# Second output projection of a two-layer encoder: where the normalisation's factors and offsets are loaded, and where the last row block's transposes stand

## The chip, the cores and the metric

One core of a Trainium2 chip. TensorE (PE) multiplies matrices and transposes blocks, VectorE (DVE), ScalarE (ACT) and GpSimd (POOL) do the element work, SyncE (SP) issues transfers. The metric is the device time of one execution in microseconds (us); the time of a kernel is the median over its runs.

## The reference

A trunk of two layers over 1024 frames with 1024 features, all in float32. Layer 0 mixes tokens by latent attention, layer 1 by differential attention; each mixer is followed by a normalised residual, then a SwiGLU feed-forward part (hidden size 2816) with another.

```python
def _swiglu(x, w_gu, w_down):
    gate, up = jnp.split(x @ w_gu, 2, axis=-1)
    return (jax.nn.silu(gate) * up) @ w_down

for i in range(DEPTH):              # DEPTH = 2
    mix = ...                       # i = 0: latent attention; i = 1: differential attention,
                                    # 8 heads, o normalised per head, then o @ w_o
    h = _layernorm(ALPHA * h + mix, ln_mix_g[i], ln_mix_b[i])
    h = _layernorm(ALPHA * h + _swiglu(h, ffn_w_gu[i], ffn_w_down[i]), ln_ffn_g[i], ln_ffn_b[i])
```

The change lies at the end of layer 1's mixer: the product `o @ w_o`, the first normalisation with `ln_mix_g[1]` and `ln_mix_b[1]`, and the start of layer 1's feed-forward part.

## The kernel before

The 1024 frames are eight row blocks of 128. float32 products are made of rounded halves: an operand is split into a high and a low part (`op_unit`: a cast on ScalarE, L517, then a difference on VectorE or POOL, L518), and TensorE makes three products, high by high, high by low and low by high.

**Attention's last head and the output projection.** Attention goes head by head. Within a head and row block there are scores `s_b` (L220) for two softmax maps; `l_b` holds the logits, exponentials (L228, ScalarE) and, after the reciprocal `rb` (L1442), the scaling on POOL (L1443) and the difference of the two maps (L1444, VectorE), the attention weights. These are transposed by TensorE into `pt_b` (L148), split into `pth_b` and `ptl_b` (L251, L252), and multiplied with the values into `o_b` (L263). The last head takes the row blocks in the order `LAST_ORDER = (6, 7, 4, 5, 2, 3, 0, 1)`.

`OutProj` makes `o @ w_o` for these blocks. Its constructor loads the split weights of the eight heads: `who`/`wlo` for heads 0 and 1 (L376), and one tile `wo_2` to `wo_7` of 1 MB each for the others (L370), all from SP. `of` loads the transposed `o` of six heads for a block (L388), `load_z` the residual `z_a` (L412). For blocks 6 and 7 the product `zp_a` (L431) with heads 0 to 5 runs early, between the last head's rows; the rest runs when that head is done. `rest` normalises each block with `gb`, a tile that holds factors and offsets broadcast to all 128 partitions (0.5 MB each; L176 multiplies by the factors, L184 adds the offsets), and then `raw_x` transposes the block into the feed-forward part's operand (`xTp_a`, eight 128x128 transposes per block in two tiles). The last block's `raw_x` is returned by `rest` as a function, and is called by the feed-forward part.

**The start of the feed-forward part.** Its first products are the gate columns: `load` fetches gate operands `gp_n` from SP (L577) and combined ones `gr_n` (L571), `prepare` and `op_unit` make operands of them, and `consume` multiplies: product "1" then "2" of column group n into the accumulator `ga_n` (L561). After "1" ScalarE copies the accumulator (L628), after "2" it applies SiLU (L630), and the accumulator's bank is free for another group; ga_2 takes that of ga_0.

**What sets the order.** The program is written in dependency order, and a scheduler that works with planned durations of instructions and transfers sets the order on every engine; each engine then executes its list in order. `behind(i, j)` adds a bare order: instruction i is planned behind j. A queue on SP executes its issues in order; each transfer has a semaphore out of a ring of eight, so an issue can wait for the transfer eight issues back.

Of the kernel before, what the change touches and what calls it, by code (L numbers as in the profile page):

```python
# [16 lines left out]
P = 128  # L17
# [21 lines left out]
LAST_ORDER = (6, 7, 4, 5, 2, 3, 0, 1)  # L39
# [3 lines left out]
def trunk(  # L43
# [32 lines left out]
    nc = tc.nc  # L76
    V, A, G, T = nc.vector, nc.scalar, nc.gpsimd, nc.tensor
# [4 lines left out]
    ident = cp.tile([P, P], F32, tag="ident", name="ident")  # L82
# [24 lines left out]
    def f32(t):  # L107
        return t.bitcast(F32)

    def big_tile(name, dt=F32R):  # L110
        return big.tile([P, 2, 1024], dt, tag="big", name=name)

    def ps_s(name):
        return ps.tile([P, 512], F32, tag="s", bufs=ps_bufs[0], name=name)

    def ps_m(name):
        return ps.tile([P, 512], F32, tag="m", bufs=ps_bufs[1], name=name)
# [27 lines left out]
            T.matmul(ps_out, ll, rh, start=False, stop=(i == n - 1))  # L145

    def tr(ps_out, in_):
        T.transpose(ps_out, in_, ident)  # L148

    def bcast_row(pool, src, n, name, tag):  # L150
        t = pool.tile([P, n], F32, tag=tag, name=name, bufs=1)
# [3 lines left out]
    def behind(i, j):  # L155

        tc.add_manual_dep(
            i, j.name,
            mybir.DependencyInfo(mybir.DependencyClass.NoSync, mybir.DependencyReason.DATA),
            reason="kept in program order",  # L160
        )
# [46 lines left out]
    ends = {}  # L208
# [140 lines left out]
    class OutProj:  # L349
# [5 lines left out]
        def __init__(self, side, w_dr, o_dram, o_here, x_src, x_dst, scale):  # L355
            self.st = ExitStack()
            self.pool = self.st.enter_context(tc.tile_pool(name="op1", bufs=2, side=side, reuse_waits="tile"))
            self.o_dram, self.o_here, self.x_src, self.x_dst, self.scale = o_dram, o_here, x_src, x_dst, scale
            self.oh, self.z, self.sums, self.m, self.loaded = {}, {}, {}, {}, {}
            self.of(LAST_ORDER[0])  # L360
            self.wo = []
            for h in range(H):
                if h == 6:
                    self.load_z(LAST_ORDER[0])
                if h == self.HEADS:
                    self.of(LAST_ORDER[1])
                    self.load_z(LAST_ORDER[1])
                if h > 1:
                    t = self.pool.tile([P, 2, D], F32, tag=f"wo{h}", name=f"wo1_{h}", bufs=1)
                    nc.sync.dma_start(t, w_dr[h])  # L370
                    t = t.bitcast(F32R)
                    self.wo.append((t[:, 0], t[:, 1]))
                else:
                    t = [wp.tile([P, D], F32, tag=f"w{p}", name=f"w{p}o1_{h}") for p in "hl"]
                    for p in range(2):
                        nc.sync.dma_start(t[p], w_dr[h][:, p])  # L376
                    self.wo.append([x.bitcast(F32R) for x in t])
# [80 lines left out]
        def rest(self, lng, lnb, xo):  # L458
            gb = big_tile("gb1", F32)
            for i, src in enumerate((lng, lnb)):  # L460
                nc.gpsimd.dma_start(gb[:, i], src.partition_broadcast(P))
            prev = None
            for tb in LAST_ORDER:
                if tb not in LAST_ORDER[:2]:
                    self.of(tb)
                if tb != LAST_ORDER[0]:
                    self.late(tb)
                z = self.z[tb]
                layer_norm(z, self.sums[tb], [self.m[tb, nh] for nh in range(2)], z, gb[:, 0], gb[:, 1],
                           f"a1_{tb}", self.x_dst[tb * P:(tb + 1) * P, :])  # L470
                if prev is not None:
                    raw_x(self.z[prev], xo, prev, f"a1_{prev}")
                prev = tb
            self.st.close()
            return lambda: raw_x(self.z[prev], xo, prev, f"a1_{prev}")

    def raw_x(y, xo, tb, name):

        c = slice((tb % 4) * P, (tb % 4) * P + P)
        pvs = []
        for kh in range(2):
            pt = ps_s(f"xTp_{name}_{kh}")
            for k in range(4):
                tr(pt[:, k * P:(k + 1) * P], y[:, (4 * kh + k) * P:(4 * kh + k + 1) * P])
            pv = pt.rearrange("p (k t) -> p k t", k=4)
            pvs.append(pv)
            if tb >= 4:
                hi, lo = (t[:, :, c] for t in xo[kh, 0])  # L490
                A.copy(hi, pv)
                V.tensor_tensor(lo, pv, f32(hi), ALU.subtract)
                A.copy(xo["r", kh, 0][:, :, c], pv)
        if tb < 4:
            b11, b12, b21, b22 = (xo["r", k, t][:, :, c] for k in range(2) for t in range(2))
            V.tensor_tensor(b12, pvs[0], b11, ALU.subtract)
            A.copy(b22, pvs[1])
            V.tensor_tensor(b11, b22, pvs[0], ALU.subtract)
            V.tensor_tensor(b21, b21, pvs[1], ALU.subtract)
            ends["x"] = V.tensor_tensor(b21, b21, b12, ALU.add).ins  # L500
# [33 lines left out]
    def ffn(side, xo, xst, pending, layer, x_src, x_dst, lng, lnb, next_x, spare=()):  # L534
# [15 lines left out]
        r, tmp, ops, acc, hp, pg, early_cast = {}, {}, {}, {}, {}, {}, {}  # L550
        pg_dr = dr.tile([npre // 2, P, 4, 512], F32, name=f"pg_dr{layer}")

        def p1g0(n):


            t, i = (tmp[n], 2) if n in tmp and n > 1 else (pg[n // 2], 2 * (n % 2))
            return t[:, i], t[:, i + 1]

        def product(o, w, x, first):
            return [  # L560
                T.matmul(  # L561
                    o, w[:, a, k * P:(k + 1) * P], x[b][:, k, :], start=(first and k == 0 and (a, b) == (0, 0)),
                    stop=(k == 3 and a == 1), skip_group_check=True,
                ).ins for k in range(4) for a, b in ((0, 0), (0, 1), (1, 0))
            ]
# [50 lines left out]
        def consume(n, pr):  # L616


            w, nm_ = ops.pop((n, pr)), f"{layer}_{n}"
            if pr in "12":  # L620
                if pr == "1":
                    acc[n, "a"] = ps_s(f"ga{nm_}")
                    if n >= npre:
                        new_tmp(n)
                product(acc[n, "a"], w, xo["12".index(pr), 0], pr == "1")
                p1, g0 = p1g0(n)
                if pr == "1":
                    ends["p1"] = A.copy(p1, acc[n, "a"]).ins  # L628
                else:
                    A.activation(g0, acc[n, "a"], AF.Silu)  # L630
                return
            if pr in "53":
                if pr == "5" or n < 2:
                    acc[n, "c"] = c = (ps_s if n == 1 else ps_t)(f"gc{nm_}{pr}")
                    acc.setdefault((n, "cs"), []).append(c)
                i = product(acc[n, "c"], w, xs["t1" if pr == "5" else "b22"], pr == "5" or n < 2)
                if n == NFF - 1 and pr == "5":
                    behind(i[0], ends["7"])
                if n < 2:
                    return  # L640
            else:
                if pr == "6":
                    acc[n, "b"] = ps_m(f"gb{nm_}")
                    if n < npre:
                        new_tmp(n)
                ends[pr] = product(acc[n, "b"], w, xs[{"6": "t2", "7": "t3", "4": "t4"}[pr]], pr == "6")[-1]
            u2, u3 = tmp[n][:, 0], tmp[n][:, 1]
            p1, g0 = p1g0(n)
            if pr == "6":
                V.tensor_tensor(u2, p1, acc[n, "b"], ALU.add)  # L650
                for c in acc[n, "cs"] if n < 2 else ():
                    V.tensor_tensor(u2, u2, c, ALU.add)
            elif pr == "7":
                V.tensor_tensor(u3, p1, acc[n, "b"], ALU.add)
                if n < 2:
                    V.tensor_tensor(u3, u3, acc[n, "cs"][0], ALU.add)
            elif pr == "5":
                V.tensor_tensor(u3, u3, acc[n, "c"], ALU.add)
            elif pr == "4":
                V.tensor_tensor(p1, p1, acc[n, "b"], ALU.add)  # L660
            else:
                V.tensor_tensor(u2, u2, acc[n, "c"], ALU.add)
            if n == NFF - 1 and pr == "3":
                held.append((n, u2, u3, p1, g0))
            elif pr == ("4" if n < 2 else "3"):
                activations(n, u2, u3, p1, g0)
# [360 lines left out]
        else:  # L1027
            gb = big_tile(f"gb_{nm}", F32)
# [11 lines left out]
            for t in range(4):  # L1040
                y = yb[t // 2][:, t % 2]
# [4 lines left out]
            for t in range(4):  # L1046
                y = yb[t // 2][:, t % 2]
# [297 lines left out]
    xo, stacks = x_pools("m0", "right")  # L1345
# [16 lines left out]
    with ExitStack() as st:  # L1362
# [11 lines left out]
        for ql in q_lo:  # L1374
            for mp in range(2):
                b = slice(64 - mp * 64, 128 - mp * 64)
                z = bb[b, :512]
                i = G.tensor_tensor(ql[b, mp * 512:mp * 512 + 512], z, z, ALU.subtract).ins
# [169 lines left out]
    xo, stacks = x_pools("m1", "left")  # L1548
# [92 lines left out]
```

## Time and profile before

| | us |
|---|---|
| median of 3 runs (2258.09 to 2258.78) | 2258.73 |
| the profiled execution's own time | 2259.4 |
| its span in the profile | 2257.6 |
| TensorE busy | 2236.1 |
| VectorE, ScalarE, POOL busy | 1543.2, 1013.5, 773.6 |
| mean granted TensorE clock, share of full | 0.999 |

The profile's rows carry engine, line, operation and tile, written out<-in; numbers that tell apart the tiles of one name are left out (`wo` is wo_2 to wo_7). "Idle before, <-releaser" is the time for which an engine waited ahead of an instruction, and what ended it. PEld is TensorE's loading of weights, which overlaps its products. q1 is the queue of transfers that SP issues, q0 that of POOL's.

### The profile page before, as it was taken

How to read it: one execution, taken by the hardware profiler on the slowest of the kernel's cores; microseconds unless marked ns; L12 is line 12 of the kernel's file. 1: busy time of each engine (PE TensorE's matmuls, PEld its weight loads, DVE VectorE, ACT ScalarE, POOL GpSimd, SP SyncE). 2: the span in 40 equal slices, each digit the busy share in tenths (PEclk: the TensorE clock that was granted, in tenths of full speed). 3: DMA queues.
4: the chain of work that ended last, by engine and by line, in shares of the span. 5: the costliest groups of instructions: out<-in, count | busy, mean ns of one | idle time of the engine just before them, and what ended most of it. 6: DMA issues, size and time to landing. Idle time of an engine off the chain costs nothing.

```text
span 2257.6 us, 31061 instructions
## 1 busy us (share of the span) xinstructions
PE 2236.1 (99%) x11410; PEld 1912.8 (85%) x11410; DVE 1543.2 (68%) x2894; ACT 1013.5 (45%) x2097; POOL 773.6 (34%) x626
## 2 busy tenths in 40 slices
PE   8999999999999999999999999999999999999998
PEld 8999998888888888888889898988888888888886
DVE  5676765696666657767576666577787666658778
ACT  4455664352333334445465656455532333334444
POOL 2232341114434440456432424222014444430561
PEclk9999999999999999999999999999999999999999
DMA  5010125434435338454311212063344232238443
GB/s 204 14 35 32 42 71 187 142 129 148 178 126 204 118 131 326 177 200 150 103 44 33 64 34 68 24 224 131 121 150 163 80 113 98 103 114 324 164 182 149
DMA packets 105545, 287.76 MB, mean 127 GB/s; under 512 B 7968, under 2 KB 30112, under 8 KB 94896
## 3 DMA queue, kind: packets, MB, share of 16 engines
q1 hardware_dynamic: 101552, 277.44, 34.5%
q0 software_dynamic: 3840, 8.33, 1.4%
q8 instruction: 90, 1.47, 0.3%
q14 instruction: 63, 0.52, 0.1%
HBM read 204.47 MB, written 77.07 MB: 125 GB/s over the span
## 4 chain that ended last, share of the span: by engine, by line
PE 96%; DVE 1%; ACT 1%; DMA 1%; issue 0%; POOL 0%; SPq 0%; DVEq 0%; POOLq 0%
PE gb L561 16%; PE gc L561 10%; PE ga L561 10%; PE dw L885 8%; PE dx L885 5%; PE zp_a L431 4%; PE s_a L220 4%; PE s_b L220 3%; PE dv L885 3%; PE dy L885 3%; PE bp L145 3%; PE bp L143 3%; PE bp L144 3%; PE o_a L263 2%; PE o_b L263 2%; PE hq L1136 2%
## 5 line engine op out<-in xcount | busy, mean ns | idle before, releaser
L517 ACT CAST op_g<-gr 128x512 fp32r<-128x512 f32 x240 | 146.7, 621 | 378.3 <-PE gb L561 190.0
L518 POOL TENSOR_TENSOR op_g<-gr,op_g 128x512 fp32r<-128x512 f32 x104 | 145.9, 1408 | 254.5 <-ACT op_g L517 142.1
L518 DVE TENSOR_TENSOR op_h<-rh,op_h 128x512 fp32r<-128x512 f32 x152 | 140.6, 951 | 51.5 <-ACT op_h L517 51.5
L561 PE MATMUL ga<-xh_m,op_g 128*128 128x512 f32 x512 | 168.3, 389 | 0.0
L885 PE MATMUL dw<-op_w_t,op_h 128*128 128x512 f32 x660 | 151.1, 390 | 0.0
L517 ACT CAST op_h<-rh 128x512 fp32r<-128x512 f32 x152 | 91.9, 619 | 127.6 <-PE dx L885 35.3
L885 PEld LDWEIGHTS dw<-op_w_t,op_h 128*128 128x128 f32 x660 | 123.7, 188 | 25.6
L228 ACT ACTIVATE l_b<-l_b,mx_b 128x256 f32<-128x256 f32 (+7 forms) x128 | 99.4, 777 | 74.8 <-DVE mx_b L223 73.0
L518 POOL TENSOR_TENSOR op_w_b<-rw_b,op_w_b 128x512 fp32r<-128x512 f32 x44 | 64.4, 1486 | 172.6 <-ACT op_w_b L517 172.6
L518 DVE TENSOR_TENSOR op_g<-gr,op_g 128x512 fp32r<-128x512 f32 x136 | 111.7, 824 | 17.3 <-ACT op_g L517 17.0
L885 PE MATMUL dx<-op_w_b,op_h 128*128 128x512 f32 x528 | 121.5, 390 | 1.0 <-DVE op_w_b L518 1.0
L1443 POOL TENSOR_SCALAR l_b<-l_b,rb,cst 128x128 f32<-128x128 f32 (+3 forms) x64 | 52.5, 821 | 200.6 <-DVE rb L1442 189.2
L885 PEld LDWEIGHTS dx<-op_w_b,op_h 128*128 128x128 f32 x528 | 98.8, 188 | 23.0 <-DVE op_w_b L518 2.6
L561 PE MATMUL gb<-t2h_f,op_g 128*128 128x512 f32 x352 | 115.5, 390 | 0.4 <-DVE op_g L518 0.4
L561 PE MATMUL gc<-t1h_f,op_g 128*128 128x512 f32 x352 | 115.7, 390 | 0.0
L561 PE MATMUL gb<-t4h_f,op_g 128*128 128x512 f32 x352 | 115.6, 389 | 0.0
L561 PE MATMUL gc<-b22h_f,op_g 128*128 128x512 f32 x352 | 115.4, 389 | 0.0
L561 PE MATMUL gb<-t3h_f,op_g 128*128 128x512 f32 x352 | 115.2, 389 | 0.0
L561 PEld LDWEIGHTS ga<-xh_m,op_g 128*128 128x128 f32 x512 | 96.1, 188 | 20.0
L518 POOL TENSOR_TENSOR op_g<-s,op_g 128x512 fp32r<-128x512 f32 x40 | 55.0, 1375 | 166.3 <-ACT op_g L517 158.3
L143 PE MATMUL bp<-xT_f,h_wb 128*128 128x512 f32 x256 | 101.9, 398 | 0.0
L144 PE MATMUL bp<-xT_f,h_wb 128*128 128x512 f32 x256 | 101.6, 397 | 0.0
(388 smaller groups left out, 6690.7 us busy)
## 6 DMA issues: line engine op xcount, KB each, us to landing
gr<-in_w_gu SPq DMA_DIRECT2D x44, 1024.0 KB, 6.8
rh<-h_dr SPq DMA_DIRECT2D x28, 1024.0 KB, 5.0
h_dr<-sh SPq DMA_DIRECT2D x22, 1024.0 KB, 5.0
h_dr<-hp SPq DMA_DIRECT2D x22, 768.0 KB, 4.1
tt<-in_w_dn SPq DMA_DIRECT2D x22, 512.0 KB, 7.4
rh<-h_dr SPq DMA_DIRECT2D x12, 768.0 KB, 4.3
wo_dr<-op_pwo SPq DMA_DIRECT2D x16, 512.0 KB, 3.4
z<-xs_dr SPq DMA_DIRECT2D x16, 512.0 KB, 10.4
```

Of the source, the lines that this page charges most:

```text
L143: T.matmul(ps_out, lh, rh, start=(i == 0), stop=False)
L144: T.matmul(ps_out, lh, rl, start=False, stop=False)
L145: T.matmul(ps_out, ll, rh, start=False, stop=(i == n - 1))
L220: T.matmul(s[:, :w], lh, rh[:, ks], start=(j == 0), stop=(j == len(q_pass) - 1))
L228: ends["exp"] = A.activation(l[:, :n], l[:, :n], AF.Exp, bias=mx, scale=-1.0, accum_out=sm).ins
L263: T.matmul(po[:, c], a, b[:, j % 2, c], start=st, stop=sp_, skip_group_check=True)
L431: T.matmul(m, a[:, h, :], self.wo[h][w][:, c], start=(start and h == heads[0] and a is oh and w == 0), stop=(stop and h == heads[-1] and a ...
L517: turns["cast"] = A.copy(hi, src).ins
L518: return eng.tensor_tensor(lo, src, f32(hi), ALU.subtract).ins
L561: T.matmul(o, w[:, a, k * P:(k + 1) * P], x[b][:, k, :], start=(first and k == 0 and (a, b) == (0, 0)), stop=(k == 3 and a == 1), skip_gro ...
L885: T.matmul(o, h[:, a, c], w[:, b_], start=(first and (a, b_) == (0, 0)), stop=(last and a == 1), skip_group_check=True,).ins for a, b_ in ...
L1443: G.tensor_scalar(l1[:, :n], l1[:, :n], r[:, 1:2], nlam, ALU.mult, ALU.mult)
```

## The change

Two things. The two loads of `gb` are issued by SP instead of POOL, planned behind the load of the last weight, which the constructor keeps in `last_w`. And the transposes of the last block in `LAST_ORDER` (block 1) are planned behind the last product of gate group 0, product "2", which `consume` keeps in `ends["gate"]`.

```diff
     def tr(ps_out, in_):
-        T.transpose(ps_out, in_, ident)
+        return T.transpose(ps_out, in_, ident).ins
...
-                    nc.sync.dma_start(t, w_dr[h])
+                    self.last_w = nc.sync.dma_start(t, w_dr[h]).ins
...
         def rest(self, lng, lnb, xo):
             gb = big_tile("gb1", F32)
             for i, src in enumerate((lng, lnb)):
-                nc.gpsimd.dma_start(gb[:, i], src.partition_broadcast(P))
+                behind(nc.sync.dma_start(gb[:, i], src.partition_broadcast(P)).ins, self.last_w)
...
             for k in range(4):
-                tr(pt[:, k * P:(k + 1) * P], y[:, (4 * kh + k) * P:(4 * kh + k + 1) * P])
+                i = tr(pt[:, k * P:(k + 1) * P], y[:, (4 * kh + k) * P:(4 * kh + k + 1) * P])
+                if tb == LAST_ORDER[-1]:
+                    behind(i, ends["gate"])
...
-                product(acc[n, "a"], w, xo["12".index(pr), 0], pr == "1")
+                i = product(acc[n, "a"], w, xo["12".index(pr), 0], pr == "1")[-1]
+                if (n, pr) == (0, "2"):
+                    ends["gate"] = i
```

`raw_x` and `consume` serve both layers. The order of layer 0 and of all up to layer 1's last head is the same before and after; the scheduler makes another order of that head's end and of the start of the second feed-forward part. The last block's transposes stand in both orders between ga_0's product "2" and ga_1's.

On SP, at the output weights (the first number after a name is that of the head or row block). Before:

```order
L412 DMA z_a_7_14972<-xs_dr_98 128x1024
L370 DMA wo_6_14975<-wo_dr_95 128x2048
L370 DMA wo_7_14977<-wo_dr_96 128x2048
L388 DMA of_a_4_15581<-o_dr_2_87 128x6x128
L388 DMA of_a_5_15672<-o_dr_2_87 128x6x128
L412 DMA z_a_4_15584<-xs_dr_98 128x1024 x2
```

After; the two loads of `gb` stand between the last weight and the first load of `o`:

```order
L412 DMA z_a_7_14972<-xs_dr_98 128x1024
L370 DMA wo_6_14975<-wo_dr_95 128x2048
L370 DMA wo_7_14977<-wo_dr_96 128x2048
L461 DMA gb_15518<-in_ln_mix_g 128x1024
L461 DMA gb_15518<-in_ln_mix_b 128x1024
L388 DMA of_a_4_15581<-o_dr_2_87 128x6x128
L388 DMA of_a_5_15672<-o_dr_2_87 128x6x128
```

Both wait for semaphores of transfers only, those of wo_2 and wo_3; the two `of` loads behind them now wait for those of wo_4 and wo_5.

On TensorE, at the end of the last head, where block 3's attention weights are transposed. Before:

```order
L220 MATMUL s_b_1_1_0_15377<-bk_10192,bq_10189 128x256
L220 MATMUL s_b_1_1_0_15377<-bk_10192,bq_10190 128x256
L148 MATMUL pt_b_3_0_15386<-ident,l_b_3_0_15262 128x128 x4
L431 MATMUL zp_a_6_0_6_15467<-wo_6_14975,oh_a_6_14948 128x512 x2
L431 MATMUL zp_a_6_1_6_15475<-wo_6_14975,oh_a_6_14948 128x512 x2
L1474 MATMUL ms_2_0_15395<-sq_2_15363,ones 128x256
```

After; the transposes of block 3 are now followed by two short instructions, and the output products come behind those:

```order
L220 MATMUL s_b_1_1_0_15377<-bk_10192,bq_10189 128x256
L220 MATMUL s_b_1_1_0_15377<-bk_10192,bq_10190 128x256
L148 MATMUL pt_b_3_0_15386<-ident,l_b_3_0_15262 128x128 x4
L1478 MATMUL ms_2_0_15395<-sq_2_15363,ones 128x256
L148 MATMUL pt_b_0_0_15414<-ident,l_b_0_0_15334 128x128
L431 MATMUL zp_a_6_0_6_15467<-wo_6_14975,oh_a_6_14948 128x512 x2
```

Further up, the 18 products of `zp_a` for block 7's first half now stand ahead of that block's transposes `pt_b_7_0`; before, behind them.

On ScalarE at the same place, the exponentials of block 3 and the cast of block 2's transposes. Before:

```order
L228 ACTIVATE l_b_3_0_15262,smb_3_15260<-l_b_3_0_15262,mx_b_3_0_0_15266 128x512
L1477 ACTIVATE sq_3_15258<-ms_3_0_15293,cst 128x256
L251 CAST pth_b_4_1_15238<-pt_b_5_0_15279 128x2x128
L228 ACTIVATE l_b_3_1_15269,smb_3_15260<-l_b_3_1_15269,mx_b_3_1_0_15273 128x512
L1479 ACTIVATE sq_3_15258<-sq_3_15258 128x256
L251 CAST pth_b_2_0_15355<-pt_b_2_0_15351 128x2x128
```

After; the cast of `pt_b_2_0` comes ahead of the second exponential of block 3:

```order
L228 ACTIVATE l_b_3_0_15262,smb_3_15260<-l_b_3_0_15262,mx_b_3_0_0_15266 128x512
L1483 ACTIVATE sq_0_15169<-sq_0_15169 128x512
L1481 ACTIVATE sq_3_15258<-ms_3_0_15293,cst 128x256
L251 CAST pth_b_2_0_15355<-pt_b_2_0_15351 128x2x128
L228 ACTIVATE l_b_3_1_15269,smb_3_15260<-l_b_3_1_15269,mx_b_3_1_0_15273 128x512
L1483 ACTIVATE sq_3_15258<-sq_3_15258 128x256
```

On ScalarE at the start of the second feed-forward part. Before:

```order
L628 COPY pg_0_16137<-ga_0_16163 128x512
L628 COPY pg_0_16137<-ga_1_16177 128x512
L517 CAST op_gp_3_1_16219<-gp_3_16217 128x512
L630 ACT_TABLE_LOAD
L630 ACTIVATE pg_0_16137<-ga_0_16163 128x512
L517 CAST op_gp_3_2_16222<-gp_3_16217 128x512
L497 COPY xr_m_15515<-xTp_a_1_1_16234 128x4x128
L517 CAST t1h_f_16303<-xr_m_15517 128x512 x4
L517 CAST op_gp_4_1_16320<-gp_4_16318 128x512
```

After; the first cast of gp_4 stands ahead of the table load and ga_0's SiLU, where it stood behind the four casts of t1h:

```order
L632 COPY pg_0_16137<-ga_0_16163 128x512
L632 COPY pg_0_16137<-ga_1_16177 128x512
L519 CAST op_gp_3_1_16219<-gp_3_16217 128x512
L519 CAST op_gp_4_1_16320<-gp_4_16318 128x512
L634 ACT_TABLE_LOAD
L634 ACTIVATE pg_0_16137<-ga_0_16163 128x512
L519 CAST op_gp_3_2_16222<-gp_3_16217 128x512
L499 COPY xr_m_15515<-xTp_a_1_1_16234 128x4x128
```

On SP there, the load of gp_4 now stands ahead of those of gr_0 and gr_1, and behind them before.

## The prediction

> **What bounds the kernel now.** I read the page first, for which engine sets the end; then TensorE's waits around the change; then the stretches, the queues and the single rows there. The page, with columns of busy us, share of the span and instructions, and below it the chain that ended last:
>
> ```profile
> span 2257.6 us, 31061 instructions
> PE 2236.1 (99%) x11410; PEld 1912.8 (85%) x11410; DVE 1543.2 (68%) x2894; ACT 1013.5 (45%) x2097; POOL 773.6 (34%) x626
> PE 96%; DVE 1%; ACT 1%; DMA 1%; issue 0%; POOL 0%; SPq 0%; DVEq 0%; POOLq 0%
> ```
>
> TensorE is idle for 2257.6 − 2236.1 = 21.5 us of the whole program, so no change that leaves its instructions alone can win more. Next, its waits from 1480 to 1700 us, the second output projection and the start of the second feed-forward part, where the change acts (us in total, times, longest):
>
> ```profile
> PE zp_a L431 <- DMA wo<-wo_dr: 1.2, 1, 1.2
> PE pt_b L148 <- DVE l_b L1444: 1.2, 2, 0.9
> PE zp_a L431 <- DVE ol_a L420: 0.4, 1, 0.4
> ```
>
> Four stalls of 2.8 us together: that is the most that can be gained here. One, 1.2 us, is a wait for an output weight. The stretches round it (us, then busy us of PE, PEld, DVE, ACT, POOL, then clock, DMA share, GB/s):
>
> ```profile
> 1490.00:1496.00 6.00, 6.00 (x38) 5.24 (x36) 5.75 (x16) 4.17 (x10) 2.32 (x3) 1.00 0.94 349
> 1496.00:1500.00 4.00, 2.82 (x13) 2.03 (x12) 1.84 (x5) 1.00 (x2) 0.00 (x0) 1.00 1.02 427
> 1500.00:1510.00 10.00, 10.00 (x66) 8.89 (x65) 7.40 (x22) 5.68 (x13) 2.11 (x2) 1.00 1.02 424
> ```
>
> The transfer engines are full from 1490 on, and where TensorE stalls, VectorE and ScalarE starve too (1.84 and 1.00 of 4 us). So a stall removed here moves the whole tail of the attention forward.
>
> **The change part by part: the factors and offsets.** The issues on SP and POOL (start, duration, queue, line), the transfers' packets between 1490.0 and 1497.8, the times to landing of `gb` and of the first wide weight (wo_2, issued 1488.49), and the stall:
>
> ```profile
> 1488.49 2.01 SPq L370 DMA_DIRECT2D wo<-wo_dr  x4
> 1497.83 9.05 SPq L388 DMA_DIRECT2D of_a<-o_dr  x2
> 1490.59 0.59 POOL L461 DMA_DIRECT2D gb<-in_ln_mix_g  x1 [5.78 <-PE bv L145]
> 1491.18 0.54 POOL L461 DMA_DIRECT2D gb<-in_ln_mix_b  x1
> ...
> q1 hardware_dynamic: 430, 2.40, 81.6%
> q0 software_dynamic: 116, 0.48, 14.8%
> gb<-in_ln_mix_g POOLq DMA_DIRECT2D x1, 512.0 KB, 9.1
> gb<-in_ln_mix_b POOLq DMA_DIRECT2D x1, 512.0 KB, 12.2
> ...
> wo<-wo_dr SPq DMA_DIRECT2D x1, 1024.0 KB, 9.3
> ...
> 1497.81 0.74 PE L431 MATMUL zp_a<-wo,oh_a 128*128 128x512 f32 x2 [1.18 <-DMA wo<-wo_dr]
> ```
>
> wo_2 lands at 1488.5 + 9.3 = 1497.8, just when TensorE starts again. In the 7.8 us before, `gb` took 0.48 MB, or 14.8% of 7.8 us = 1.15 us of all 16 engines. Behind the last weight it takes none of that, so wo_2 lands 1.15 us sooner and the stall of 1.18 us all but goes: −1.15 us. Ends: 0 if wo_2 doesn't land sooner, −1.2 if the stall goes altogether. The later weights gain more (all of `gb`, 1.05 MB at 424 GB/s, is 2.5 us), so the next one isn't what is late then.
>
> [...]
>
> What the two issues pass: POOL loses 1.13 us of issuing, in an idle stretch (5.78 us idle before it): nothing. On SP they come behind wo_7 and, as each reuses the semaphore of the transfer eight issues back, wait for wo_2 and wo_3 to land; behind them stand the two `of` loads, issued from 1497.83 before, now some 6 us later. The landing time of the first `of` load, and the first uses of `of` and of `gb`:
>
> ```profile
> of_a<-o_dr SPq DMA_DIRECT2D x1, 384.0 KB, 17.9
> ...
> 1534.31 0.94 ACT L419 ACTIVATE oh_a<-of_a,cst 128x768 fp32r<-128x768 f32 x1
> ...
> 1543.99 1.28 DVE L176 SCALAR_TENSOR_TENSOR z_a<-z_a,nmu_a,gb 128x1024 f32<-128x1024 f32 x1
> ```
>
> The engines are full and the bytes the same, so the last of them lands when it did before, at about 1497.8 + 17.9 = 1515.7; some 18 us are left for `of`, 28 us for `gb`. Nothing on the path. If that cover were gone, each us of lateness would be a us of VectorE, then of TensorE.
>
> **The order of the attention's tail.** The schedule is made anew: the last head's rows stand otherwise. First a row of such products for their pace (2.89 us for 12), then the stalls that are there, and the chain that feeds the largest (l_b_3: exponential, reciprocal, POOL's scaling, VectorE's difference):
>
> ```profile
> 1613.80 2.89 PE L431 MATMUL zp_a<-wo,oh_a 128*128 128x512 f32 x12
> ...
> 1512.29 0.63 PE L148 MATMUL pt_b<-ident,l_b 128*128 128x128 f32 x4 [0.30 <-DVE l_b L1444]
> 1531.70 0.52 PE L148 MATMUL pt_b<-ident,l_b 128*128 128x128 f32 x3
> 1535.12 0.66 PE L148 MATMUL pt_b<-ident,l_b 128*128 128x128 f32 x4 [0.85 <-DVE l_b L1444]
> 1537.99 0.50 PE L431 MATMUL zp_a<-wo,ol_a 128*128 128x512 f32 x1 [0.41 <-DVE ol_a L420]
> ...
> 1531.85 0.74 ACT L228 ACTIVATE l_b<-l_b,mx_b 128x512 f32<-128x512 f32 x1
> 1533.05 0.77 POOL L1443 TENSOR_SCALAR l_b<-l_b,rb,cst 128x512 f32<-128x512 f32 x1 [1.52 <-DVE rb L1442]
> 1533.86 1.21 DVE L1444 SCALAR_TENSOR_TENSOR l_b<-l_b,rb,l_b 128x512 f32<-128x512 f32 x1 [0.15 <-POOL l_b L1443]
> ```
>
> At pt_b_7_0 (1512.29) the 18 products of zp_a_7_0 now stand ahead of it, 18 × 0.24 = 4.3 us: the stall of 0.30 goes. At pt_b_3_0 ScalarE now takes the cast of pt_b_2_0 ahead of l_b_3's second exponential; so that exponential starts some 0.75 us behind pt_b_2_0's start (0.5 for its transposes, 0.25 for the cast), and pt_b_3_0 follows 1535.12 − 1531.85 = 3.27 us behind the exponential: 4.0 us. TensorE had 1535.12 − 0.85 − 1531.70 = 2.57 us of work between the two, and has two more score products now, 2.8 us. Stall 1.2 us; up to 2.1 if other work in ScalarE's queue delays the exponential further. pt_b_2_0 itself has less ahead of it: 0 to 0.5 us. The 0.41 stays. Net −0.30 − 0.85 + (1.2 to 2.1) + (0 to 0.5): I take +0.5, near the middle; the ends are −1.15, if both old stalls go and none comes, and +1.45.
>
> **The start of the feed-forward part.** The hold on block 1's transposes sets them behind ga_0's second product, where they stood. Their input is ready at 1623.95 and they start at 1625.58 with no idle time: 0. But around them ScalarE's cast of gp_4 moves from behind the block's casts to ahead of its table load and ga_0's SiLU. Row by row: the block's normalisation and transposes, SP's issue of gp_4, ScalarE, VectorE's first use of a gr load, TensorE where ga_1 ends and ga_2 begins, and the landing times of all six gp (min, median, max), then that of gp_3:
>
> ```profile
> 1622.67 1.28 DVE L184 SCALAR_TENSOR_TENSOR z_a<-z_a,rs_a,gb 128x1024 f32<-128x1024 f32 x1
> 1625.58 1.03 PE L148 MATMUL xTp_a<-ident,z_a 128*128 128x128 f32 x8
> 1622.82 0.33 SPq L577 DMA_DIRECT2D gp<-in_w_gu  x1
> 1624.18 1.28 ACT L630 ACT_TABLE_LOAD   x1
> 1625.78 0.60 ACT L630 ACTIVATE pg<-ga 128x512 f32<-128x512 f32 x1 [0.32 <-PE ga L561]
> 1629.35 0.62 ACT L517 CAST op_gp<-gp 128x512 fp32r<-128x512 f32 x1
> 1630.53 0.69 DVE L598 TENSOR_TENSOR gr<-gr 128x512 f32<-128x512 f32 x1
> 1628.96 0.61 PE L561 MATMUL ga<-xh_m,op_gp 128*128 128x512 f32 x2
> ...
> DMA to landing us min/median/max: 3.7/4.9/6.7
> ...
> gp<-in_w_gu SPq DMA_DIRECT2D x1, 512.0 KB, 4.4
> ```
>
> gp_4 can't be issued before 1622.82 (SP waits there for VectorE to free its buffer). If it lands at L, the cast, the table load and the SiLU end at L + 0.05 + 0.62 + 1.28 + 0.60 + 0.05 = L + 2.6. ga_2 takes ga_0's accumulator, which that SiLU frees, and TensorE wants it with the second product of the row at 1628.96, at 1629.2. gp_3 had a wide gr load right behind it, as gp_4 has now, so I take its 4.4 us: L = 1627.2, ga_2 at 1629.8, stall 0.6 us. Ends: 3.7 gives none, 6.7 gives 2.9. The two gr loads, once ahead of gp_4, now go behind it, from about 1623.2; VectorE takes the first at 1630.53, 7.3 us on, and what it does ahead of that waits for gp_4's cast by then, so a late gr costs VectorE a little and TensorE nothing yet.
>
> [...]
>
> **Sum.** −1.15 + 0.5 + 0.6 = −0.05 us. The profiled execution took 2259.4 us for its span of 2257.6, 0.67 over the median of 2258.73; taken from the median, 2258.7 us. The ends add up to −1.2 − 1.15 + 0 = −2.35 and 0 + 1.45 + 2.9 = +4.35, that is 2256.4 to 2263.1.
>
> **The rivals.**
> - The weight's wait goes and nothing takes its place: gp_4 lands within 3.8 us, and the tail costs nothing or gains. −1.15, to −2.35 with the old stalls gone: 2256.4 to 2257.6. For it: a landing of 3.7. Against: five of six gp landings are longer.
> - The move does nothing, because wo_2 lands no sooner: +0.5 + 0.6, 2259.8. Against it: the DMA share of 0.94 to 1.02.
> - Slower: ScalarE stands at gp_4's cast, and ga_2 with it. It decides from L = 1626.6, a landing of 3.8 us. With the slowest, 6.7: −1.15 + 0.5 + 2.9 = +2.25, 2261.0. To be slower by over 0.2%, which is 4.5 us and about what a measurement of this kernel tells from no change, it takes a landing of 8.9 us. Only if gp_4's share goes to the gr load behind it is that possible.
>
> **How the numbers follow.** The forecast, two small stalls for one: 0.52. Nothing in its place: 0.22. No effect on wo_2: 0.12. The cast's stall at over 2 us: 0.12, of which 0.05 beyond 0.2%. Some other stall removed, more than I see: 0.02. Faster by over 0.2% has nearly no room, since all stalls here are 2.8 us: 0.02. Slower by over 0.2%: the 0.05 and another 0.02 for a wait that I did not find in the new order: 0.07. Within 0.2%: 0.91. The range takes the low end less 0.2 for the scatter, and leaves out the last us of the high end, where three bad ends must meet: 2256.2 to 2262.1.
>
> **What would show it.** In the trace after: no wait on wo in zp_a, wo_2 landing in about 8.2 us; `gb` issued by SP at about 1496 and 1500; no stall at pt_b_7_0, a larger one at pt_b_3_0; ScalarE idle ahead of the cast of gp_4, and a wait of ga on ScalarE's SiLU of some 0.6 us. I am wrong if wo_2 still stalls TensorE, if the tail after 1500 differs by over 1.5 us, or if another wait of over 2 us appears.

## The result: 3.7 us slower, and the profile after

The changed kernel takes 2262.2 us (median of 22 runs, 2260.14 to 2263.01), the kernel before 2258.46 us beside it (22 runs, 2257.08 to 2259.49). The ratio is 1.0015, with a 95% interval of 1.0009 to 1.0021: slower, but by less than the 0.2% that I took as the least that tells. The forecast was 2258.7, and its range ended at 2262.1, 0.1 us below what was measured. The profiled execution of after took 2263.01 us, with a span of 2261.2.

The head of its page (span and instructions; then per engine busy us, share, instructions):

```profile
span 2261.2 us, 31052 instructions
PE 2238.5 (99%) x11410; PEld 1912.8 (85%) x11410; DVE 1544.2 (68%) x2894; ACT 1013.6 (45%) x2097; POOL 773.3 (34%) x624
```

Against before, the span grew by 3.6 us and TensorE's busy time by 2.4 us, with the same 11410 instructions. So idle time alone, the currency of my whole prediction, explains only 1.2 of the 3.6 us.

From 1480 to 1700 us, where before had four stalls of 2.8 us, after has seven of 4.4 us. Their rows, in time order (start, duration, shape, in brackets the idle time ahead and what ended it), the last two each with the product that follows:

```profile
1496.42 0.73 PE L431 MATMUL zp_a<-wo,oh_a 128*128 128x512 f32 x2 [0.57 <-DMA wo<-wo_dr]
1530.49 0.52 PE L148 MATMUL pt_b<-ident,l_b 128*128 128x128 f32 x3 [0.97 <-DVE l_b L1448]
1533.81 0.50 PE L220 MATMUL s_b<-bk,bq 128*128 128x256 f32 x2 [0.44 <-DVE mx_b L223]
1534.88 0.66 PE L148 MATMUL pt_b<-ident,l_b 128*128 128x128 f32 x4 [0.57 <-DVE l_b L1448]
1535.87 1.22 PE L1478 MATMUL ms<-sq,ones 128*128 128x256 f32 x2 [0.34 <-ACT sq L1472]
1631.28 0.50 PE L563 MATMUL ga<-xh_m,op_gp 128*128 128x512 f32 x1 [0.87 <-ACT pg L634]
1631.62 0.40 PE L563 MATMUL ga<-xl_m,op_gp 128*128 128x512 f32 x1
1673.02 0.47 PE L563 MATMUL gb<-t3h_f,op_g 128*128 128x512 f32 x1 [0.65 <-ACT op_g L519]
1673.33 0.40 PE L563 MATMUL gb<-t3l_f,op_g 128*128 128x512 f32 x1
```

The last four rows also show that a stall costs more than its idle time. In a row of products each starts some 0.23 us after the one ahead of it (before, at 1613.80: 12 in 2.89 us, with the whole record of the last), though the record of each lasts 0.39 us. Behind the two stalls the second product starts 0.34 and 0.31 us after the first; and the idle time is counted only from the end of the last record ahead, 0.39 us after its start, while a row would have gone on after 0.23. From start to start the two stalls cost 1.16 us for 0.87 of idle time, and 0.90 for 0.65: about a quarter of a microsecond on top.

To place the loss without any model of idle time I numbered TensorE's products in both traces (they are the same 11410) and compared the starts of the n-th. Product 8000 stands just ahead of the output weights, 8100 between the waits for them and the stalls of the attention's tail, 8400 behind that tail, 8800 and 9200 in the gate columns. Where the table says half, a stretch at half clock lies in the tail (explained below it):

| kernel | idle gaps over 0.1 us, 8000 to 8400 | clock there | later than before, 8000 to 8100 | 8100 to 8400 | 8400 to 8800 | 8800 to 9200 |
|---|---|---|---|---|---|---|
| before | 4, 2.74 us | full | 0 | 0 | 0 | 0 |
| after | 6, 2.99 us | half for 3.41 us | −0.57 | +2.63 | +1.16 | +0.90 |
| r1: only the loads moved | 3, 1.56 us | full | −1.42 | −0.04 | 0 | 0 |
| r2: and the tail's new order | 7, 3.18 us | full | −0.46 | +1.19 | 0 | 0 |
| r12: r2's kernel once more | 6, 2.99 us | half for 3.41 us | −0.65 | +2.63 | 0 | +0.89 |
| r3: r1 and the gate's new order | 4, 2.11 us | full | −0.88 | −0.03 | +1.27 | 0 |
| r5: r1 and gp_4 first on SP | 4, 2.13 us | full | −0.72 | −0.02 | 0 | 0 |
| r6: after's order, loads on POOL | 7, 3.96 us | half for 3.41 us | +0.86 | +2.60 | +1.26 | +0.90 |
| r7: after without the hold | 6, 2.96 us | full | −0.67 | +1.19 | +1.28 | +1.81 |
| r8: after once more | 6, 3.02 us | half for 3.41 us | −0.76 | +2.62 | +1.24 | +1.45 |

After gains 0.6 us at the weights and loses 4.7 us in three places. (The executions also differ where the change doesn't act: the others of the table stand 0.4 to 2.1 us ahead of before's at product 8000, after's 1.0, and lose up to 0.6 us behind 9200, after's 0.6.)

**The tail's half clock.** TensorE's busy time in four stretches of the tail that follow the boundaries of the granted clock (us, PE busy, then clock, DMA share, GB/s):

```profile
1529.07:1532.48 3.41, 2.33 (x16) 1.00 0.00 0
1532.48:1535.90 3.42, 2.08 (x15) 1.00 0.16 49
1535.90:1539.31 3.41, 3.41 (x9) 0.50 1.01 378
1539.31:1542.72 3.41, 3.41 (x22) 1.00 0.84 340
```

The third stretch runs at half clock: TensorE is busy all the while, and makes 9 instructions where the next makes 22 (not all of one size). This is the busy time that isn't work. The stretch ahead of it has three of the new stalls, and TensorE was busy for 2.08 of 3.42 us. Before, on the boundaries that its own clock record gives, the stretch with the least work in the tail has 2.54 us, and the clock stayed at 1.00:

```profile
1531.24:1534.66 3.42, 3.03 (x24) 1.00 0.00 0
1534.66:1538.07 3.41, 2.54 (x13) 1.00 0.80 305
```

**The weights.** SP's issues, and the times to landing of `gb` and of the first wide weight:

```profile
1487.49 2.07 SPq L370 DMA_DIRECT2D wo<-wo_dr  x4
1496.45 0.33 SPq L461 DMA_DIRECT2D gb<-in_ln_mix_g  x1
1498.90 0.33 SPq L461 DMA_DIRECT2D gb<-in_ln_mix_b  x1
...
gb<-in_ln_mix_g SPq DMA_DIRECT2D x1, 512.0 KB, 15.9
...
wo<-wo_dr SPq DMA_DIRECT2D x1, 1024.0 KB, 8.9
```

The loads stand where I said, behind the last weight. wo_2 lands after 8.9 us instead of 9.3, and its stall falls from 1.18 to 0.57 us: half of the gain that I counted.

**The gate columns.** The cast of gp_4 on ScalarE, and the load's time to landing:

```profile
gp<-in_w_gu SPq DMA_DIRECT2D x1, 512.0 KB, 4.7
...
1628.70 0.62 ACT L519 CAST op_gp<-gp 128x512 fp32r<-128x512 f32 x1 [3.47 <-DMA gp<-in_w_gu]
1629.34 1.28 ACT L634 ACT_TABLE_LOAD   x1
1630.63 0.60 ACT L634 ACTIVATE pg<-ga 128x512 f32<-128x512 f32 x1
```

ScalarE stands for 3.47 us at the cast; the table load and ga_0's SiLU come behind it, and ga_2 waits 0.87 us for the SiLU. That is the term that I priced at 0.6 us.

The third place, product 8866 at 1673.02, is not in the prediction. It starts with a later SiLU, whose result SP stores, and the load of gr_3 behind that store. The two issues, first before, then after, and there also SP's waits for stores from 1640 to 1665 us (us in total, times, longest):

```profile
1654.49 0.33 SPq L707 DMA_DIRECT2D pg_dr<-pg  x1
1658.71 2.31 SPq L571 DMA_DIRECT2D gr<-in_w_gu  x2
```

```profile
1657.40 0.33 SPq L711 DMA_DIRECT2D pg_dr<-pg  x1
1661.66 1.98 SPq L573 DMA_DIRECT2D gr<-in_w_gu  x2
...
SPq L573 <- DMA pg_dr<-pg: 6.9, 2, 3.5
```

SP issues the load only when the store has landed. Both come 2.9 us later than before. TensorE itself is 2.2 us late by then; the other 0.7 us is the new order of the gate columns, in which this SiLU's products end 0.7 us later. gr_3 lands at 1666.6, VectorE waits for it, and a later operation of VectorE's runs beside one of POOL's (VectorE's and POOL's rows of after):

```profile
1666.68 0.69 DVE L600 TENSOR_TENSOR gr<-gr 128x512 f32<-128x512 f32 x1 [1.08 <-DMA gr<-in_w_gu]
1671.02 1.26 DVE L600 TENSOR_TENSOR gr<-gr 128x512 f32<-128x512 f32 x1
1672.20 0.67 DVE L654 TENSOR_TENSOR tmp<-pg,gb 128x512 f32<-128x512 f32 x1
...
1670.44 1.30 POOL L520 TENSOR_TENSOR op_g<-s,op_g 128x512 fp32r<-128x512 f32 x1 [46.21 <-ACT op_g L519]
```

VectorE's operation of 0.69 us takes 1.26 us while POOL's runs; `tmp`, which frees the accumulator that product 8866 needs, starts at 1672.20 and takes 0.67 us, and the product follows at 1673.02. (TensorE's row names a cast there; it had long been done.)

### The profile page after: what moved, and what is told of

It reads as the page before. It is cut to its first block, busy times and chain, and to the rows that moved or that the text cites. A ratio compares the mean times of both kernels' runs of the same rounds, so it can differ in the third digit from the quotient of the medians.

```text
span 2261.2 us, 31052 instructions
## 1 busy us (share of the span) xinstructions
PE 2238.5 (99%) x11410; PEld 1912.8 (85%) x11410; DVE 1544.2 (68%) x2894; ACT 1013.6 (45%) x2097; POOL 773.3 (34%) x624
## 4 chain that ended last, share of the span: by engine, by line
PE 95%; DVE 2%; ACT 1%; DMA 1%; POOL 1%; issue 0%; SPq 0%; DVEq 0%; POOLq 0%; ACTq 0%
PE gb L563 16%; PE gc L563 10%; PE ga L563 10%; PE dw L889 8%; PE dx L889 5%; PE zp_a L431 4%; PE s_a L220 3%; PE s_b L220 3%; PE dv L889 3%; PE dy L889 3%; PE bp L145 3%; PE bp L143 3%; PE bp L144 3%; PE o_a L263 2%; PE o_b L263 2%; PE hq L1140 2%
```

## The experiments

The two halves of the change and their side effects can be taken apart if the order is fixed. In the kernels called pinned, a table gives for each engine and SP the instructions from the last head on in the wanted order, and each is planned behind the one ahead of it in the table, with a bare order and no wait. Each kernel was compared with the kernel before in the same session.

### Which part costs

**r1**, the loads on SP as in the change, and before's order on every engine:

```diff
+PINNED = [[14997, 14998, 15029, 15002, 15003, 15030, 15031, ...], ...]
...
-                    nc.sync.dma_start(t, w_dr[h])
+                    self.last_w = nc.sync.dma_start(t, w_dr[h]).ins
...
-                nc.gpsimd.dma_start(gb[:, i], src.partition_broadcast(P))
+                behind(nc.sync.dma_start(gb[:, i], src.partition_broadcast(P)).ins, self.last_w)
...
+        made = {i.name: i for blk in nc.cur_f.blocks for i in blk.instructions}
+        for ids in PINNED:
+            for p, q in zip(ids, ids[1:]):
+                tc.add_manual_dep(
+                    made[f"I-{q}"], f"I-{p}",
+                    mybir.DependencyInfo(mybir.DependencyClass.NoSync, mybir.DependencyReason.DATA), reason="pinned",
+                )
```

> The factors and offsets load on SP behind the last weight, and every engine keeps the order of the kernel before (the order is written out by hand for the stretch that changed). Theory A, that the new order and not the load costs the time: the weight's stall shrinks from 1.18 us to 0.6 or less, the two stalls on pt_b stay, TensorE's clock never halves, and the time is 0.6 to 1.2 us under that of before. Rival B, that the load itself does the harm: as slow as the changed kernel, 3.7 us over before.

2257.74 us (11 runs) against 2258.86, −1.1 us; ratio 0.9994 (0.9985 to 1.0003). Its waits of TensorE from 1480 to 1700:

```profile
PE pt_b L253 <- DVE l_b L1549: 1.1, 2, 0.9
PE zp_a L536 <- DVE ol_a L525: 0.4, 1, 0.4
```

Here the wait for the weight is gone altogether and nothing takes its place (−1.42 us in the table). The time agrees with my term of −1.15, but its interval includes no change.

**r2**, r1 with after's order up to the end of the attention's tail:

```diff
-        14997, 14998, 15029, 15002, 15003, 15030, 15031, 15032, 15033, 15034, 15035, 15058, 15059, 15298, 15299, 
+        14997, 14998, 15029, 15002, 15003, 15298, 15299, 15300, 15304, 15305, 15306, 15030, 15031, 15032, 15033, 
...
```

> As r1, but the last head's end stands in the changed kernel's order; the start of the feed-forward part stands as before. [...] 2.1 us over before with the half clock, 0.4 us without it, so a median between +0.4 and +2.1 us. Rival B, that this order costs nothing: as r1.

2260.17 us (11), +1.3; ratio 1.0005 (0.9996 to 1.0014). So the tail's order costs 2.4 us against r1. In its profile the four new stalls are there, they cost 1.2 us (products 8100 to 8400), and the clock stays full, which leaves the difference open between stalls alone and stalls with a clock that falls in some executions.

**r3**, r1 with after's order at the gate columns alone:

```diff
-        16259, 16260, 16261, 16262, 16263, 16264, 16265, 16266, 16267, 16268, 16269, 16270, 16343, 16344, 16272, 
+        16259, 16260, 16261, 16262, 16263, 16264, 16265, 16266, 16267, 16268, 16269, 16270, 16343, 16344, 16345, 
...
```

> As r1, but the start of the feed-forward part stands in the changed kernel's order (gp_4's cast ahead of the table load, its load ahead of both gr loads). Theory A: the wait of ga_2 for ga_0's SiLU is there (1.2 us later from there on), and the 0.9 us that the changed kernel lost at 1672 us too: 1.0 to 1.5 us over before. Rival B, that the 0.9 us belongs to that one execution: 0 to 0.6 us over before.

2259.27 us (11), +0.4; ratio 1.0002 (0.9994 to 1.0011), 1.5 us over r1. In its profile the wait of ga for the SiLU, 0.93 us, is new, beside one of 0.56 us for the weight, which r1 alone is without. The stall at product 8866 is not there, so the time missed the 1.0 to 1.5 us over before of theory A and lies in the range of its rival.

**r6**, after's order everywhere with the loads left on POOL:

```diff
+PINNED = [[14997, 14998, 15029, 15002, 15003, 15298, 15299, ...], ...]
...
                 nc.gpsimd.dma_start(gb[:, i], src.partition_broadcast(P))
```

> The load stays on POOL's queue, as before the change, but every engine keeps the changed kernel's order. Theory A, that the order costs and the load gains: the wait for the weight is there at 1.2 us or more, and the time is 0.5 to 1.2 us over the changed kernel, 4.2 to 5 us over before. Rival B, that load and order only cost together: at before's time.

2263.82 us (10), +5.2; ratio 1.0023 (1.0014 to 1.0033), 1.4 us over after, somewhat more than I had expected. The weights' stall is back at its old size, and the next weight is late too:

```profile
1497.58 0.74 PE L536 MATMUL zp_a<-wo,oh_a 128*128 128x512 f32 x2 [1.18 <-DMA wo<-wo_dr]
1504.36 0.73 PE L536 MATMUL zp_a<-wo,oh_a 128*128 128x512 f32 x2 [0.35 <-DMA wo<-wo_dr]
```

So the move of the loads is worth 1.1 us in before's order and 1.4 us in after's by the times; in the table r6 and after also differ by 1.4 us at the weights. By differences of medians the parts are −1.1 (loads), +2.4 (tail) and +1.5 (gate columns), +2.8 in all, against 3.7 measured. The 0.9 us left over has the size of the stall at product 8866, which r3's profile doesn't have and after's has. Each of these differences is small against the intervals; that they are the same places as in the traces is what carries them.

### Why the tail costs more than its idle time

**r8**, after unchanged, once more, so that there is no edit. Either the half clock comes again at the same product, or, if it doesn't belong to that place, it may be missing, and the tail is then 1.3 to 1.7 us shorter:

> [...] Rival B, that the half clock belongs to this place in the program: it is there again at the same matrix product.

2262.61 us, one execution. The tail's stalls are the same to 0.01 us (that at product 8866 is longer, 1.16 us), and there is again a half clock, behind a stretch with as little work:

```profile
1532.00:1535.41 3.41, 2.06 (x12) 1.00 0.32 96
1535.41:1538.82 3.41, 3.41 (x11) 0.50 0.94 353
```

The half clock begins at product 8238 in after and at 8239 here, so this run leaves open whether it belongs to that place.

**r12**, r2's kernel once more and again without an edit, for whether the same instructions meet the half clock in one execution and not in another; I had expected 2.1 us over before with it and 0.7 without:

> [...] Rival B, that the half clock needs the changed kernel's start of the feed-forward part too: none.

2262.07 us, one execution. Stretches of r12, then of r2:

```profile
1533.09:1536.50 3.41, 2.06 (x13) 1.00 0.26 83
1536.50:1539.91 3.41, 3.41 (x11) 0.50 0.89 321
```

```profile
1533.36:1536.77 3.41, 2.06 (x11) 1.00 0.43 144
1536.77:1540.18 3.41, 3.41 (x19) 1.00 0.96 376
```

One kernel lost 2.63 us between products 8100 and 8400 with the half clock and 1.19 without. The table has nothing between: 2.60 to 2.63 in the four executions with the half clock, 1.19 in the two with the same stalls at full clock (r2, r7), and −0.04 to −0.02 where the tail keeps before's order. So the stalls by themselves cost 1.2 us and the half clock 1.4 us on top, a little less than half of 3.41 us. The half clock belongs neither to this place in the program alone nor to the new start of the feed-forward part, which r12 doesn't have. r2 also shows the limit of what I can say: its stretch of 60% was followed by full clock.

**r4**, after's order with 16 products added in front of the four stalls (7, 3, 4 and 2). Their results are overwritten, so they are pure load:

```diff
+            if (tb, nh, heads[0]) == (LAST_ORDER[0], 0, self.HEADS):
+                for _ in range(16):
+                    T.matmul(m[:, :256], oh[:, 0, :], self.wo[2][0][:, :256], start=True, stop=True, skip_group_check=True)
```

> The changed kernel with 16 more matrix products of 256 columns (some 0.12 us each, 1.9 us in all), whose results are overwritten, placed where TensorE waits: 7 ahead of pt_b_2_0, 3 ahead of s_b_1_1, 4 ahead of pt_b_3_0, 2 ahead of ms_2. All else keeps the changed kernel's order. [...]

If the idle time at these stalls brings the half clock, I had expected none of it and 1 to 1.7 us under after; if something else does, 0 to 1.9 us over after. 2260.94 us (11), +2.1; ratio 1.0011 (1.0002 to 1.0019). With 1.9 us more work it is not slower than after but, by medians against before, 1.7 us faster (the intervals overlap). From product 8100 to the same work behind the tail it loses 1.25 us against before, about what r2 and r7 lose there at full clock. The clock stays full in the stretches that were short of work, in the one execution that was profiled:

```profile
1530.33:1533.74 3.41, 3.21 (x23) 1.00 0.00 0
1533.74:1537.15 3.41, 3.21 (x19) 1.00 0.62 211
```

**r9** and **r10** split the filling: r9 only the nine products at the three later stalls, r10 only the seven ahead of the first.

```diff
-                for _ in range(16):
+                for _ in range(9):
```

> As r4, with 9 of the 16 extra products only: 3 ahead of s_b_1_1, 4 ahead of pt_b_3_0, 2 ahead of ms_2. [...]

```diff
-                for _ in range(16):
+                for _ in range(7):
```

> As r4, with the other 7 products only, ahead of pt_b_2_0, the longest stall (0.97 us). [...]

If the three later stalls bring the half clock, I had expected none of it and 2.0 to 2.5 us over before for r9, and for r10 the half clock and 3.3 to 3.9 us; if all four stalls share in it, 2.6 to 3.2 us for both.

r9 2260.98 us (11), +2.4, ratio 1.0012 (1.0004 to 1.0021); r10 2261.65 (11), +3.1, ratio 1.0012 (1.0003 to 1.0021). Neither profile has a half clock. For r9 that is what the first case said, for r10 it isn't: its one profile has the three later stalls, of 0.6, 0.4 and 0.3 us, at full clock, and the time lies in the range of the second. The medians stand in the order that the three later stalls as the cause would give, but the intervals overlap: which of the stalls matters most isn't settled.

### The gate columns

**r5**, r1 with only the transfers' new order, gp_4's load ahead of those of gr on SP, and ScalarE's cast where it stood before:

```diff
-        16218, 16226, 16228, 16319, 16105, 16335, 
+        16218, 16319, 16226, 16105, 16228, 16335, 
```

> As r1, but gp_4's load stands ahead of both gr loads on SP, as in the changed kernel; ScalarE, VectorE and TensorE keep the order of before, with gp_4's cast behind the SiLU and the block's casts. Theory A, that the cast ahead of the SiLU is what costs at the start of the feed-forward part, and not the transfers' order: no wait of ga for a SiLU, 0 to 0.5 us over r1. Rival B, that the late gr loads cost it: 1 to 1.5 us over r1, as r3.

2257.22 us (11) against 2258.66, −1.4; ratio 0.9995 (0.9986 to 1.0004). No wait of ga; the three lines are all that TensorE waits for from 1480 to 1700:

```profile
PE pt_b L253 <- DVE l_b L1549: 1.1, 2, 0.9
PE zp_a L536 <- DMA wo<-wo_dr: 0.6, 1, 0.6
PE zp_a L536 <- DVE ol_a L525: 0.4, 1, 0.4
```

So the order of the transfers is free, and what costs is what r3 moves besides. That includes other pieces of the engines' orders, and no run moves the cast alone; the trace names it: ScalarE stands at it for 3.47 us in after and 3.5 in r3, and ga_2 waits for the SiLU behind it.

**r7**, after without its second half, the hold on the last block's transposes:

```diff
-                i = tr(pt[:, k * P:(k + 1) * P], y[:, (4 * kh + k) * P:(4 * kh + k + 1) * P])
-                if tb == LAST_ORDER[-1]:
-                    behind(i, ends["gate"])
+                tr(pt[:, k * P:(k + 1) * P], y[:, (4 * kh + k) * P:(4 * kh + k + 1) * P])
```

> The load's half of the change alone: the transposes of the last block are not held, and the scheduler sets them 12 products earlier, ahead of ga_0's product "2", with the block's casts ahead of the SiLU. Theory A, that TensorE pays for each place where it meets an operand that isn't there: some 1.0 us of waiting for the block's normalisation and a wait of ga_2 for the SiLU that is longer by the casts (2.7 us): 2 to 4 us over the changed kernel. Rival B, that the hold does nothing, since it leaves the transposes where they were before: the changed kernel's time.

2262.3 us (11), +3.6; ratio 1.0016 (1.0007 to 1.0025). I had expected 2 to 4 us over after, and it is after's time, as the rival said. The transposes do come too early without the hold, and wait for the block's normalisation; but then ga_2 no longer waits:

```profile
1623.97 1.06 PE L148 MATMUL xTp_a<-ident,z_a 128*128 128x128 f32 x8 [1.08 <-DVE z_a L184]
...
PE gb L561 <- DVE tmp L650: 1.5, 1, 1.5
```

A stall of 1.08 us takes the place of one of 0.87, and that at product 8866 is larger. With the half clock missing in this one profile, the hold looks worth up to a microsecond there; the times show no difference.

### A version that tries for more

**r11**, r1 with the one piece of after's tail order that I had counted as a gain, the 18 products of `zp_a` ahead of `pt_b_7_0`:

```diff
-        15070, 15071, 15301, 15302, 15303, 15307, 15308, 15309, 15075, 15076, 15126, 15127, 15152, 15153, 15154, 
+        15070, 15071, 15301, 15302, 15303, 15307, 15308, 15309, 15075, 15076, 15126, 15127, 15421, 15422, 15423, 
...
```

> r1 with one thing of the new order that gained: the 18 products of zp_a_7_0 stand ahead of pt_b_7_0. The stall of 0.27 us there goes, and the time is 0.1 to 0.5 us under r1, 1.2 to 1.7 us under before. Rival: the products wait for wo_5 there and give it back, as r1.

2260.05 us (11), +1.5; ratio 1.0006 (0.9998 to 1.0015). A miss: the stall of 0.27 us goes, and the products that took its place wait for their accumulator, which VectorE has still to read; two shorter stalls, of 0.36 and 0.29 us, follow:

```profile
1510.92 0.50 PE L536 MATMUL zp_a<-who,oh_a 128*128 128x512 f32 x1 [0.78 <-DVE z_a L544]
```

The versions that beat both kernels by their medians are r1 and r5, 1.1 and 1.4 us under before; against after their intervals lie apart from its own, against before they include no change.

## Why the prediction was wrong, point by point

- **The weights, −1.15: near the mark in the times, about half in most traces.** r1 gave −1.1 and r6 against after 1.4. With the loads on POOL wo_2 lands after 9.3 and 9.5 us (before, r6), with the loads on SP after 8.5 to 9.0 us and in r1 after 8.0. So the `gb` bytes that wo_2 no longer shares with brought it 0.3 to 0.8 us in most profiles, not 1.15, and its stall falls to 0.54 to 0.58 us (after, r2, r3, r5, r7, r8, r12), only in r1's to nothing. What I had put aside, a late second weight, is a part of what the move saves in after's order (0.35 us in r6). The two pairs of kernels that differ in the loads' queue gave 1.1 and 1.4 us. Before, 116 packets of q0 moved among 430 of q1 in the 7.8 us ahead of wo_2's landing; in after only q1's did (539 from 1488 to 1496).
- **What the two issues pass: right.** `gb` comes 6 and 8 us later on SP, the first `of` 3.6 us and not 6, and neither shows up among the waits.
- **The tail, +0.5: the step that failed.** The term priced each stall at its idle time and took TensorE's pace outside the stalls as fixed. By the starts of products 8100 to 8400 the new order cost 1.19 us in the two executions of it at full clock, and 2.60 to 2.63 us in the four in which the clock halved behind the stalls. The first is what the short stalls cost with the slow start behind each, and is within my upper end of +1.45; the 1.4 us of half clock had no place in the sum, and with it the tail, +2.4 us in the times, is beyond that end. The idle time did come out near my figure, but by luck. The 0.30 and the 0.85 went as I had said; the 0.41 that was to stay went too; pt_b_3_0 waits 0.57 us and not 1.2 to 2.1; pt_b_2_0 0.97 and not 0 to 0.5; and 0.44 and 0.34 are at places that I hadn't named. That makes 2.32 us in place of 1.56, +0.76, because the errors largely cancel.
- **The start of the feed-forward part, +0.6: the mechanism right, the size short.** gp_4 landed after 4.7 us, not 4.4, and was issued a microsecond later, as all that comes behind the tail was; the wait was 0.87 us, and with the slow start behind it the part cost 1.2 us in the traces and 1.5 in the times.
- **The late gr "costs VectorE a little and TensorE nothing yet": wrong, 43 us on.** Late is gr_3, not the first two: its load waits for a store to land, and the store for a SiLU that the new gate order makes 0.7 us later. It costs 0.9 us in after and 1.45 in r8. All seven profiles with the new orders of tail and gate columns have this stall (r4, r9, r10 and, without the hold, r7 too), r3 with the new gate order alone has not, and of the six with before's gate order only r12 has it. r12 and r2 are the same kernel. VectorE's wait for gr_3 in each, r12 then r2, with the time to landing of the store ahead of the load:

```profile
1665.83 0.69 DVE L703 TENSOR_TENSOR gr<-gr 128x512 f32<-128x512 f32 x1 [0.88 <-DMA gr<-in_w_gu]
...
pg_dr<-pg SPq DMA_DIRECT2D x1, 1024.0 KB, 5.0
```

```profile
1663.55 0.69 DVE L703 TENSOR_TENSOR gr<-gr 128x512 f32<-128x512 f32 x1 [0.28 <-DMA gr<-in_w_gu]
...
pg_dr<-pg SPq DMA_DIRECT2D x1, 1024.0 KB, 4.2
```

  So a slow store can make gr_3 too late in before's order as well, and r3, whose store landed after 3.8 us, escaped with a VectorE wait of 0.50 us. How often each happens isn't known, and that the 0.9 us left over in the times is this stall isn't shown.
- **The hold, 0: right as a step from where the transposes stood.** Taking it out of after moves the time by nothing that shows (r7).
- **The rivals.** "ScalarE stands at gp_4's cast" is what happened there, at a landing beyond its point of 3.8 us, but with a wait of 0.87 us as in the sum, not of over 2. None of the rivals had the clock, and the chance of 0.02 for "a wait that I did not find" was far too small for an order made anew at dozens of places of which I had read four.

## What to carry to other kernels

When one load is moved under a scheduler, read the whole new order on the busiest engine and price every place where its operand is made later than before; the load's own gain (1.1 us) was smaller than what the reshuffle cost (some 4 us). Here a short stall cost its idle time plus about a quarter of a microsecond, and in four of the six profiled executions with all four new stalls of the tail 3.41 us at half clock followed: look at the granted clock behind such stalls, and not at their idle time alone. If a move is worth having, pin the rest of the order, as r1 and r5 do.

## What the runs showed of the hardware

- **The clock halved behind a stretch in which TensorE was mostly busy.** In four profiles (after, r6, r8, r12) a stretch of 3.41 us with TensorE busy for 60 to 61% was followed by 3.41 us at clock 0.50; in after no gap in it was longer than 0.57 us. (In r6 the two stretches are 1535.12 to 1538.54, with 2.07 us of work, and 1538.54 to 1541.95.)

  The clock stayed full behind stretches of 3.03 and 2.54 us of work in before's tail and of 3.21 us in r4's, behind 2.18 us at r6's weights (1494.16 to 1497.57; the products behind it start 0.23 us apart), and in r2 behind 2.06 us, as much as r12, the same kernel, had ahead of its half clock. So the same kernel may or may not be hit, and what decides it isn't shown. In after the clock changes lie 1525.76, 3.41 and 716.80 us apart, which is 447, 1 and 210 times 3.4133 us.
- **An operation of VectorE's took over half a microsecond longer while one of POOL's ran.** In after VectorE's product of two operands took 1.26 us, from 1671.02, instead of 0.69, beside POOL's operation of 1.30 from 1670.44; in r12 and r8 the same operation of VectorE's took 1.24 and 1.19 us. In before POOL's took 1.58 us, from 1668.21, and VectorE's beside it the usual 0.68. What decides which of the two takes longer isn't shown. That a shift in VectorE's arrival decides whether TensorE stalls behind it is my estimate from these lengths.
